# Splitting the tokens of a mixture of experts into two short-mantissa parts, and reordering the work inside an expert

## Chip, cores and metric

One core of a Trainium2 chip runs the whole program. The metric is the device time of one execution in microseconds (us). The kernel before takes 1766.9 us, the median of three runs (1766.51 to 1769.05 us).

## What is computed

The program is two transformer blocks on 256 tokens of 1024 numbers. The change lies in the mixture of experts (MoE) of the first block. Cut to what matters here, with `T` = 256, `D` = 1024, 32 experts and 4 of them for each token:

```
h      = rms_norm(x) * gain + shift
logits = h @ w_router + b_router
top 4 experts of each token, gates = softmax of their logits
for each expert e, on the tokens that chose it:
    u = h[those] @ w_mlp1[e] + b_mlp1[e]           # 1024 x 2048
    a = min(u[even], 7) * sigmoid(1.702 * ...) * (clip(u[odd]) + 1)
    y = a @ w_mlp2[e] + b_mlp2[e]                  # 1024 x 1024
    out[those] += gate * y
x = x + gt2 * rms_norm(out)
```

An expert's weights are 12 MB, so the MoE streams 384 MB from memory.

## The kernel before, in words

All of it is one function whose instructions run on each engine in the order in which the code issues them; semaphores alone tie the engines together. TensorE (PE) multiplies, VectorE (DVE) and ScalarE (ACT) evict and do elementwise work, GpSimd (POOL) does little, and SyncE (SP) issues the weight loads.

**Weights.** They come in chunks of 1 MB, twelve for an expert: `("m1", e, k)` for k = 0 to 7 and `("m2", e, q)` for q = 0 to 3. In the MoE a list of 18 buffers holds them (`NA` 4, `NE1` 2, `ND` 4, `NC` 3, `NF2` 4, and the buffer `xb` once the transposed tokens `x1` are read, L1332). `done(key)` (L121) hands a buffer back and issues the next load at once; SP waits there until the buffer's last reader is through.

**Routing (L1309 to L1385).** The tokens are turned, the router's logits and the top 4 are found, and `q1` says for each token and expert in which of 64 slots (`CAP`) of that expert the token sits. `select` (L1213) makes 0/1 matrices from it on DVE.

**Gather.** For a group of experts, `gather_rows` (L1227) multiplies the selection, already scaled by the tokens' norm `yt` (`factored`, L1220), by the tokens `x_tok` in float32: two PSUM banks of 512 columns. `gather_half` (L1239) copies a bank on ACT, turns it with four PE transposes, and evicts with gain and shift on ACT and DVE into `xg`, two pairs of evictions for each expert. The groups are expert 0 alone (by `gather_few`, L1261), then pairs 1 and 2, 3 and 4, and so on, and expert 31 alone (L1291). Expert e does the gather of the next group when it is the last of its own (`look`), so the experts with an even number do it.

**One expert (L1540 to L1654).** In the order of PE: the bias (`up_start`); products with chunks 0 to 2 of m1, both halves `u0` and `u1` of the result (`up(0, ..)`, `up(1, ..)`); `spread`, which adds the rows of the expert before to the output; chunk 3; with `look` the gather's products; chunk 4 of both halves; the first half of the turned gather; chunks 5 to 7 of `u0`; the second half of the gather; chunks 5 to 7 of `u1`. In float32 every product of the code is two instructions on PE, and the 64-column tiles run two at a time. Then `glu` (L1423) makes `a_sb` of `u0` on DVE and ACT, `slots_of` (L1404) finds which tokens the rows belong to, `turn` (L1436) transposes `a_sb` and ACT copies it to `aT`, `glu` does `u1`, and `down_q` (L1442) multiplies by the four chunks of m2.

**Experts with more than 64 tokens.** Three conditional blocks (`tc.If(more > 0)`, L1580, L1624, L1640) do the rest; here two experts, 3 and 17, take them. Where a block isn't taken, each engine still passes it in its order, and there sets the semaphores that the block's instructions would have set. The tile `vx` (L1579) of the first two blocks, read on DVE in the second, and the tile `aT` (L1627) share one buffer:

```
            vx = P.tile([128, 512], F32, name="vx", tag="aT", bufs=1)
            ...
            glu(us, a_sb)
            ax = P.tile([128, 1, 256], F32, name="ax", tag="sely", bufs=1)
            with tc.If(more > 0):
                nc.vector.tensor_tensor(vx, vx, up_more(range(4, KD)), op=OP.add)
                glu([vx], ax)
            aT = P.tile([128, 512], F32, name="aT", tag="aT", bufs=1)
```

Of the kernel before, what the change touches and what calls it, by code (L numbers as in the profile page):

```python
# [10 lines left out]
F32 = mybir.dt.float32  # L11
F32R = mybir.dt.float32r
# [3 lines left out]
AF = mybir.ActivationFunctionType  # L16
OP = mybir.AluOpType
# [4 lines left out]
D = 1024  # L22
KD = D // 128
NE = 32
CAP = 64
MORE = 32
# [4 lines left out]
GB = 2  # L31
# [5 lines left out]
ND = 4  # L37
NF2 = 4
IN2 = (8, 0, 9, 1, 6, 2, 7, 3, 4, 5)
# [7 lines left out]
def body(ctx: ExitStack, tc: tile.TileContext, I, out, dbg=None, n_experts=NE):  # L47
    nc = tc.nc
# [31 lines left out]
    def wps(name):  # L80
        if len(banks) == 1:
            return banks["w"].tile([128, 512], F32, name=name, tag="w")

        tags = banks["tags"]
        tags.append(tags.pop(0))
        return banks["w"].tile([128, 512], F32, name=name, tag=tags[-1], bufs=1)
# [1117 lines left out]
    with ExitStack() as ph:  # L1204
# [14 lines left out]

        def factored(sel, w):  # L1220

            ys = P.tile([128, 2, w], F32, name="sely", tag="selz" if w == MORE else "sely", bufs=1)
            for b in range(2):
                nc.vector.tensor_scalar(ys[:, b], sel[:, b].bitcast(F32), yt[:, b:b + 1], None, op0=OP.mult)
            return ys

        def gather_rows(sel, w):  # L1227

            ys = factored(sel, w)
            ps = []  # L1230
            for q in range(2):
                p = wps("xrp")
                for b in range(2):
                    nc.tensor.matmul(p[0:w, :], ys[:, b], x_tok[:, b, q * 512:(q + 1) * 512], start=(b == 0),  # L1234
                                     stop=(b == 1), skip_group_check=True)
                ps.append(p)
            return ps

        def gather_half(ps, q, w, xgs):  # L1239

            xr = P.tile([128, 512], F32, name="xr", tag="yh", bufs=1)
            nc.scalar.activation(xr[0:w, :], ps[q][0:w, :], AF.Copy)  # L1242
            p = ps[q]
            for c in range(4):
# [16 lines left out]
        def gather_few(sel, w, xg):  # L1261

            ys = factored(sel, w)
            n = 128 // w
            m = D // n
            p = wps("xrp")
            for b in range(2):
                for g in range(n):
                    nc.tensor.matmul(p[w * g:w * g + w, 0:m], ys[:, b], x_tok[:, b, g * m:(g + 1) * m],
                                     start=(b == 0), stop=(b == 1), skip_group_check=True, tile_position=(0, w * g))  # L1270
            xr = P.tile([128, 512], F32, name="xr", tag="yh", bufs=1)
# [18 lines left out]

        groups = [[0]] + [list(range(e, min(e + GB, n_experts))) for e in range(1, n_experts, GB)]  # L1291

        def group_size(gi):
            return len(groups[gi])
# [36 lines left out]
        dump("x1T", x1)  # L1331
        slots.append((xpool, "xb", state["moe_end"]))  # L1332
        rt = P.tile([128, 2, NE], F32, name="rt", tag="aT")
# [37 lines left out]
        xg0 = group_tile(0)  # L1371
        gather_few(sel0[:, :, 0], CAP, xg0[0])
        cur = sel0, xg0
# [29 lines left out]

        def slots_of(e, sel, w, tg, sg):  # L1404

            pm = wps("pm")
            for b in range(2):
                for c in range(128 // w):
                    nc.tensor.matmul(pm[w * c:w * c + w, 0:2], sel[:, b, :].bitcast(F32), gt2[:, b, e, :],
                                     start=(b == 0), stop=(b == 1), skip_group_check=True, tile_position=(0, w * c))  # L1410
            nc.vector.tensor_copy(tg, pm[:, 0:2])
            nc.vector.tensor_scalar(sg, iota_t, pm[:, 0:1], None, op0=OP.is_equal)
# [79 lines left out]
        def next_slots(e, q, done):  # L1492

            nc.vector.tensor_scalar(q[:, :, e:e + 1], q[:, :, e:e + 1], -float(done), None, op0=OP.add)
            sel = select(lambda b: q[:, b, e:e + 1][:, :, None], 1, MORE, "selx", 1)[:, :, 0]
            slots_of(e, sel, MORE, tgx, sgx)
            gather_few(sel, MORE, xgx)
# [42 lines left out]
        for e in range(n_experts):  # L1540
            gi, j = (e + GB - 1) // GB, (e + GB - 1) % GB if e else 0
            look = e == groups[gi][-1] and gi + 1 < ng
# [47 lines left out]

            kb = KD - 1 if e == n_experts - 1 else 5
            for k in range(4, kb):
                up(0, (k,))
                up(1, (k,))
            if look:
                gather_half(xrs, 0, w, nxg)
            up(0, range(kb, KD))
            if look:
                gather_half(xrs, 1, w, nxg)
            up(1, range(kb, KD))  # L1600
            if e == min(BIAS_AT, n_experts - 1):
# [19 lines left out]
            sg = P.tile([128, T], F32R, name="sg", tag="sg", bufs=1)  # L1621
            glu(us, a_sb)
            ax = P.tile([128, 1, 256], F32, name="ax", tag="sely", bufs=1)
# [4 lines left out]
            for k in range(4, KD):  # L1628
                done(("m1", e, k))
            slots_of(e, sel[:, :, j], CAP, tg, sg)  # L1630
            pt = wps("apt")
            turn(a_sb, (0,), aT, pt)
            glu(us, a_sb, (1,))
            yp = wps("yp")
# [396 lines left out]
```

## Time and profile before

| | us |
|---|---|
| median of three runs | 1766.9 |
| the profiled execution | 1763.47 |
| its span, first to last instruction | 1761.7 |
| MoE, first product with w_mlp1 to last product with w_mlp2 | 193.0 to 1175.2 |
| PE busy in the span | 1641.9 (93%) |
| DVE, ACT, POOL busy | 682.7, 516.2, 17.3 |

Engine times are from one profiled execution, counted from its first instruction. PE's busy time is the time in which at least one matmul runs; matmuls overlap, so a busy PE can still have room. "Granted clock" (PEclk) is the share of full TensorE clock: 1.00 is 2.4 GHz, 0.50 is 1.2 GHz.

### The profile page before, as it was taken

The page shows a single profiled execution, that of the slowest core. Times are in us where ns is not written, and L with a number is a line of the kernel's source. Part 1 is how long each engine was busy: PE and PEld are TensorE (multiplying, and loading weights), DVE is VectorE, ACT ScalarE, POOL GpSimd, SP SyncE. Part 2 cuts the span into 40 slices and gives each one's busy share as a digit, 9 for nine tenths or more (in the row PEclk, how much of TensorE's full clock was granted, in tenths as well). Part 3 has the DMA queues.
Part 4 walks back from the last instruction along what each step waited for, and adds up shares of the span by engine and source line. Part 5 has one row for each costly group of instructions (what it writes and reads, how often), then busy time and mean ns, then how long its engine had stood idle before and what let it go on. Part 6 is the DMA issues. An engine that isn't in the chain of part 4 may idle for free. (4 is left out here: it accounts for less than half of the span.)

```text
span 1761.7 us, 25407 instructions
## 1 busy us (share of the span) xinstructions
PE 1641.9 (93%) x9983; PEld 975.6 (55%) x9983; DVE 682.7 (39%) x1444; ACT 516.2 (29%) x980; POOL 17.3 (1%) x37
## 2 busy tenths in 40 slices
PE   6998899899999799989999999979999999999997
PEld 3776332333333233233333333339999998999997
DVE  4656312212221121221212121237666765666666
ACT  2544201101110111110111011135444546554443
POOL 1000000000000000000000000000000000000000
PEclk8999899999999899999999999989999999999999
DMA  9987899799999999979999999955565653445552
GB/s 324 371 262 291 347 412 402 289 411 413 416 413 415 406 415 415 409 308 412 413 416 413 416 414 415 416 192 168 168 201 166 205 182 121 144 154 193 188 171 96
DMA packets 169750, 545.61 MB, mean 310 GB/s; under 512 B 11280, under 2 KB 90720, under 8 KB 133728
## 3 DMA queue, kind: packets, MB, share of 16 engines
q1 hardware_dynamic: 168304, 540.60, 79.9%
q8 instruction: 125, 2.05, 0.5%
q0 software_dynamic: 480, 1.58, 0.3%
q10 hardware_dynamic: 784, 0.92, 0.2%
q14 instruction: 57, 0.47, 0.1%
HBM read 542.01 MB, written 1.05 MB: 308 GB/s over the span
## 5 line engine op out<-in xcount | busy, mean ns | idle before, releaser
L1551 PE MATMUL u<-chunk,xg 128*64 128x512 f32 x2048 | 471.6, 602 | 2.2 <-PEq L1580 1.9
L1551 PEld LDWEIGHTS u<-chunk,xg 128*64 128x64 f32 x2048 | 145.7, 138 | 267.9 <-issue 253.9
L1455 PE MATMUL yp<-chunk,aT 128*64 128x512 f32 x1024 | 250.2, 633 | 18.2 <-ACT aT L1440 14.9
L448 DVE TENSOR_TENSOR ul<-chunk,uh 128x1024 fp32r<-128x1024 f32 x202 | 239.1, 1220 | 36.1 <-ACT uh L434 35.7
L434 ACT ACTIVATE uh<-chunk 128x1024 fp32r<-128x1024 f32 x202 | 205.0, 1049 | 58.7 <-DMA chunk<-in_ffn_w_up_dram 31.0
L310 PE MATMUL gu<-nhi,uh 128*128 128x256 f32 x704 | 200.1, 284 | 0.0
L310 PE MATMUL gu<-nhi,ul 128*128 128x256 f32 x704 | 199.5, 283 | 0.0
L310 PE MATMUL gu<-nlo,uh 128*128 128x256 f32 x704 | 199.5, 283 | 0.0
L1455 PEld LDWEIGHTS yp<-chunk,aT 128*64 128x64 f32 x1024 | 70.7, 142 | 147.2 <-issue 123.4
L310 PEld LDWEIGHTS gu<-nhi,uh 128*128 128x128 f32 x704 | 135.5, 192 | 1.2 <-issue 0.4
L310 PEld LDWEIGHTS gu<-nlo,uh 128*128 128x128 f32 x704 | 135.4, 192 | 0.9
L310 PEld LDWEIGHTS gu<-nhi,ul 128*128 128x128 f32 x704 | 135.4, 192 | 0.0
L1465 DVE SCALAR_TENSOR_TENSOR yl<-yp,tg,yh 128x512 fp32r<-128x512 f32 x32 | 24.0, 751 | 243.4 <-ACTq L1580 185.2
L1256 DVE TENSOR_TENSOR xg<-xrp,gs 128x128 f32<-128x128 f32 x62 | 18.1, 292 | 254.9 <-ACT xg L1251 254.9
L1430 DVE TENSOR_SCALAR g<-u 128x256 f32<-128x256 f32 x64 | 26.9, 420 | 190.1 <-PE u L1551 190.1
L1431 ACT ACTIVATE s<-g 128x256 f32<-128x256 f32 x66 | 27.5, 417 | 222.5 <-DVE g L1430 219.2
L1464 ACT ACTIVATE yh<-yp,tg 128x512 fp32r<-128x512 f32 x32 | 22.0, 687 | 164.1 <-PEq L1640 147.4
L1242 ACT ACTIVATE xr<-xrp 128x512 f32<-128x512 f32 (+1 forms) x32 | 19.0, 594 | 168.2 <-PE xrp L1234 168.2
L1251 ACT ACTIVATE xg<-xrp,modT,gs 128x64 f32<-128x64 f32 x124 | 43.3, 399 | 84.7 <-PE xrp L1245 73.9
L1440 ACT ACTIVATE aT<-apt 128x256 f32<-128x256 f32 x64 | 24.5, 383 | 143.2 <-PE apt L297 106.1
L1234 PE MATMUL xrp<-x_tok,sely 128*128 128x512 f32 (+1 forms) x128 | 58.7, 601 | 5.0 <-PEq L1580 5.0
L1142 DVE TENSOR_TENSOR gu<-gu,rs 128x512 f32<-128x512 f32 (+1 forms) x46 | 30.7, 668 | 82.7 <-PE gu L310 82.4
(465 smaller groups left out, 2331.0 us busy)
## 6 DMA issues: line engine op xcount, KB each, us to landing
chunk<-in_w_mlp_dram SPq DMA_DIRECT2D x384, 1024.0 KB, 18.9
chunk<-in_w_ada_dram SPq DMA_DIRECT2D x24, 1024.0 KB, 6.8
chunk<-in_ffn_w_gate_dram SPq DMA_DIRECT2D x22, 1024.0 KB, 5.4
chunk<-in_ffn_w_up_dram SPq DMA_DIRECT2D x22, 1024.0 KB, 7.9
chunk<-in_ffn_w_down_dram SPq DMA_DIRECT2D x22, 1024.0 KB, 6.2
chunk<-in_w_in_dram SPq DMA_DIRECT2D x17, 1024.0 KB, 5.0
chunk<-in_w_gate_dram SPq DMA_DIRECT2D x8, 1024.0 KB, 6.7
chunk<-in_w_out_dram SPq DMA_DIRECT2D x6, 1024.0 KB, 8.4
```

Of the source, the lines that this page charges most:

```text
L310: nc.tensor.matmul(ps, a, b, start=first, stop=False, skip_group_check=True)
L434: nc.scalar.activation(hi if spec is None else spec(hi), view(raw(key)), AF.Copy)
L448: nc.vector.tensor_tensor(vl, view(raw(key)), vh.bitcast(F32), op=OP.subtract)
L1142: nc.vector.tensor_tensor(gu[:, a0:a1, :], p, rs[:, None, :].to_broadcast([128, a1 - a0, T]), op=OP.mult)
L1234: nc.tensor.matmul(p[0:w, :], ys[:, b], x_tok[:, b, q * 512:(q + 1) * 512], start=(b == 0), stop=(b == 1), skip_group_check=True)
L1251: nc.scalar.activation(xg[:, k, :], at, AF.Identity, scale=gs[:, 2, k:k + 1], bias=modT[:, 24 + k:25 + k])
L1430: nc.vector.tensor_scalar(g, uv[:, :, 0], 7.0, None, op0=OP.min)
L1431: nc.scalar.activation(s, g, AF.Sigmoid, scale=1.702)
L1440: nc.scalar.activation(aT[:, r * 256:(r + 1) * 256], pt[:, r * 256:(r + 1) * 256], AF.Copy)
L1455: nc.tensor.matmul(yp[w * d:w * d + w, 0:m], a, wt[:, o:o + m], start=(q + h == 0), stop=(q + h == 4), skip_group_check=True, tile_positio ...
L1465: nc.vector.scalar_tensor_tensor(yl, yp[:, 0:m], tg[:, 1:2], yh.bitcast(F32), op0=OP.mult, op1=OP.subtract)
L1551: nc.tensor.matmul(u, xg[j][:, k, :], raw(("m1", e, k))[:, n * 512:(n + 1) * 512], start=False, stop=(k == KD - 1), skip_group_check=True, ...
```

## The change

Once the router has read them, the tokens are split: `x_hi` is a copy rounded to the short mantissa (F32R) made on ACT, and `x_lo` is the rest, subtracted on POOL. `gather_rows` takes the plain 0/1 selection times both parts, one instruction for each product, and fetches the norm `yt` of each row with tiny products; ACT multiplies by it in its copy. `gather_few` takes both parts as float32. The groups become pairs from expert 0 on, so that the first pair is gathered before the loop, and experts 1, 3, ... 29 do the others; nobody gathers in expert 30. `x_tok` gives its buffer `xa` to the weight chunks (but for the last 14), `x_hi` lies in `xb`, `NF2` falls to 3, and in the last expert POOL adds the parts to `x_tok` again. Inside an expert chunks 4 and 5 of `u0` go before the first half of the gather, chunks 6 and 7 before the second, and chunks 4 to 7 of `u1` behind it; both halves of `glu` stand before the second conditional block; and `slots_of` stands behind `turn`, in a bank of its own.

```diff
-NF2 = 4
+NF2 = 3
...
         def gather_rows(sel, w):
-            ys = factored(sel, w)
             ps = []
             for q in range(2):
                 p = wps("xrp")
-                for b in range(2):
-                    nc.tensor.matmul(p[0:w, :], ys[:, b], x_tok[:, b, q * 512:(q + 1) * 512], start=(b == 0),
-                                     stop=(b == 1), skip_group_check=True)
-                ps.append(p)
+                if q == 0:
+                    for b in range(2):
+                        nc.tensor.matmul(p[0:w, 0:1], sel[:, b].bitcast(F32), yt[:, b:b + 1], start=(b == 0),
+                                         stop=(b == 1), skip_group_check=True)
+                    yg = P.tile([128, 1], F32, name="yg", tag="yg", bufs=2)
+                    nc.vector.tensor_copy(yg[0:w, :], p[0:w, 0:1])
+                    ps.append(yg)
+                    first = p
+                else:
+                    for n, pn in ((1, p), (0, first)):
+                        for b in range(2):
+                            for x in (x_hi, x_lo):
+                                nc.tensor.matmul(pn[0:w, :], sel[:, b], x[:, b, n * 512:(n + 1) * 512],
+                                                 start=(b == 0 and x is x_hi), stop=(b == 1 and x is x_lo),
+                                                 skip_group_check=True)
+                    ps += [p, first]
             return ps
...
-            nc.scalar.activation(xr[0:w, :], ps[q][0:w, :], AF.Copy)
-            p = ps[q]
+            nc.scalar.activation(xr[0:w, :], p[0:w, :], AF.Copy, scale=yg[0:w, :])
...
-        groups = [[0]] + [list(range(e, min(e + GB, n_experts))) for e in range(1, n_experts, GB)]
+        groups = [list(range(e, min(e + GB, n_experts))) for e in range(0, n_experts, GB)]
...
-        slots.append((xpool, "xb", state["moe_end"]))
+        x_hi = xpool.tile([128, 2, D], F32R, name="x_hi", tag="xb")
+        x_lo = P.tile([128, 2, D], F32R, name="x_lo")
+        for h in (1, 0):
+            for b in range(2):
+                cs = slice(h * 512, (h + 1) * 512)
+                nc.scalar.activation(x_hi[:, b, cs], x_tok[:, b, cs], AF.Copy)
+                nc.gpsimd.tensor_tensor(x_lo[:, b, cs], x_tok[:, b, cs], x_hi[:, b, cs].bitcast(F32), op=OP.subtract)
+        slots.append((xpool, "xa", state["moe_end"] - 14))
...
-        gather_few(sel0[:, :, 0], CAP, xg0[0])
+        w = group_size(0) * CAP
+        xrs = gather_rows(sel0, w)
+        for h in range(2):
+            gather_half(xrs, h, w, xg0)
...
-            kb = KD - 1 if e == n_experts - 1 else 5
-            for k in range(4, kb):
-                up(0, (k,))
-                up(1, (k,))
-            if look:
-                gather_half(xrs, 0, w, nxg)
-            up(0, range(kb, KD))
-            if look:
-                gather_half(xrs, 1, w, nxg)
-            up(1, range(kb, KD))
+            if e == n_experts - 1:
+                for k in range(4, KD):
+                    up(0, (k,))
+                    up(1, (k,))
+                x_tok = xpool.tile([128, 2, D], F32, name="x_tok", tag="xa")
+                for b in range(2):
+                    nc.gpsimd.tensor_tensor(x_tok[:, b, :], x_hi[:, b, :].bitcast(F32), x_lo[:, b, :].bitcast(F32),
+                                            op=OP.add)
+            else:
+                up(0, (4, 5))
+                if look:
+                    gather_half(xrs, 0, w, nxg)
+                up(0, (6, 7))
+                if look:
+                    gather_half(xrs, 1, w, nxg)
+                up(1, range(4, KD))
...
-            glu(us, a_sb)
+            glu(us, a_sb, (0, 1))
             ax = P.tile([128, 1, 256], F32, name="ax", tag="sely", bufs=1)
             with tc.If(more > 0):
...
-            slots_of(e, sel[:, :, j], CAP, tg, sg)
             pt = wps("apt")
             turn(a_sb, (0,), aT, pt)
-            glu(us, a_sb, (1,))
+            pm = banks["w"].tile([128, 512], F32, name="pm", tag="u0")
+            slots_of(e, sel[:, :, j], CAP, pm)
+            slot_rows(pm, tg, sg)
             yp = wps("yp")
             down_q(yp, CAP, raw(("m2", e, 0)), 0, aT)
             turn(a_sb, (1,), aT, pt)
```

## Rows read from the trace of the kernel before

**Rows 1.** The profile page, part 1: busy us, share of the span, instructions.

```profile
PE 1641.9 (93%) x9983; PEld 975.6 (55%) x9983; DVE 682.7 (39%) x1444; ACT 516.2 (29%) x980; POOL 17.3 (1%) x37
```

**Rows 2.** Windows: us, busy (instructions) by engine, PEclk, DMA share, GB/s; experts 5, 6, 30.

```profile
359.50:384.90 25.40, 24.23 (x120) 8.49 (x120) 4.30 (x11) 2.29 (x5) 0.00 (x0) 1.00 1.01 405
384.90:418.00 33.10, 30.96 (x136) 10.44 (x136) 7.42 (x23) 6.13 (x15) 0.00 (x0) 0.95 1.01 415
...
1115.90:1145.70 29.80, 28.73 (x136) 9.70 (x136) 6.06 (x19) 4.75 (x11) 0.00 (x0) 1.00 1.02 416
```

**Rows 3.** Lines 112 (1078 to 1079 us) and 1551 (1115 to 1117 us): durations, starts.

```profile
L112 SPq DMA_DIRECT2D chunk<-in_w_mlp_dram x1: 3879/3879/3879, 1078.4 to 1078.4; - x1
...
DMA to landing us min/median/max: 21.3/21.3/21.3
...
L1551 PE MATMUL u<-chunk,xg x4: 592/592/592, 1116.3 to 1116.8; 128*64 128x512 f32 x4
```

**Rows 4.** Timeline of PE, expert 6, which gathers: start us, us, what.

```profile
393.99 3.67 PE L1234 MATMUL xrp<-x_tok,sely 128*128 128x512 f32 x8 [0.31 <-PEq L1580]
...
399.46 0.66 PE L1245 MATMUL xrp<-ident,xr 128*128 128x128 f32 x4
...
402.77 0.66 PE L1245 MATMUL xrp<-ident,xr 128*128 128x128 f32 x4
403.36 2.80 PE L1551 MATMUL u<-chunk,xg 128*64 128x512 f32 x12
...
408.66 3.56 PE L1455 MATMUL yp<-chunk,aT 128*64 128x512 f32 x8 [0.47 <-ACT aT L1440]
```

**Rows 5.** Timelines of ACT and DVE, the same expert.

```profile
401.81 0.59 ACT L1242 ACTIVATE xr<-xrp 128x512 f32<-128x512 f32 x1
...
405.79 0.42 DVE L1430 TENSOR_SCALAR g<-u 128x256 f32<-128x256 f32 x1
...
408.22 0.38 ACT L1440 ACTIVATE aT<-apt 128x256 f32<-128x256 f32 x1 [1.56 <-PE apt L297]
```

**Rows 6.** Lines 1624 and 1440, 400 to 410 us: waits of the queues (q).

```profile
L1624 DVEq EVENT_SEMAPHORE  x1: 21/21/21, 407.6 to 407.6; - x1
...
L1440 ACTq EVENT_SEMAPHORE  x1: 17/17/17, 407.7 to 407.7; - x1
```

**Rows 7.** Timeline of PE, expert 7, which does not gather.

```profile
426.98 7.09 PE L1551 MATMUL u<-chunk,xg 128*64 128x512 f32 x32 [0.16 <-PEq L1580]
...
435.75 1.94 PE L1455 MATMUL yp<-chunk,aT 128*64 128x512 f32 x8 [0.53 <-ACT aT L1440]
```

**Rows 8.** Timeline of PE and line 1036: short-mantissa products and their weight loads.

```profile
168.31 0.39 PE L1036 MATMUL y<-u,mixl 128*128 128x512 f32 x1
...
168.99 0.39 PE L1036 MATMUL y<-u,mixl 128*128 128x512 f32 x1
...
L1036 PEld LDWEIGHTS y<-u,mixl x32: 187/188/192, 146.8 to 170.8; 128*128 128x128 f32 x32
```

**Rows 9.** Windows over the second products of experts 2 and 4.

```profile
272.23:281.40 9.17, 9.17 (x34) 2.60 (x34) 0.99 (x3) 0.71 (x2) 0.00 (x0) 0.83 1.02 421
...
351.78:359.40 7.62, 7.61 (x34) 2.33 (x34) 1.00 (x3) 0.71 (x2) 0.00 (x0) 1.00 1.02 426
```

**Rows 10.** The start of the MoE (window, timeline), and POOL beside DVE at the end.

```profile
183.30:190.10 6.80, 4.14 (x13) 1.03 (x12) 2.52 (x14) 0.18 (x1) 0.00 (x0) 0.50 1.02 423
...
186.19 3.68 PE L1269 MATMUL xrp<-x_tok,sely 128*64 128x512 f32 x8 [1.73 <-DVE sely L1224]
...
193.03 1.48 PE L1551 MATMUL u<-chunk,xg 128*64 128x512 f32 x6
...
1754.35 1.44 POOL L1975 TENSOR_TENSOR o_tok<-x,fgain 128x512 f32<-128x512 f32 x1 [2.40 <-DVE x L1969]
...
1754.57 1.76 DVE L1975 TENSOR_TENSOR o_tok<-x,fgain 128x512 f32<-128x512 f32 x1
```

**Rows 11.** Groups by line and form: the gather for the experts with more tokens.

```profile
L1269 PE MATMUL xrp<-x_tok,sely 128*32 128x256 f32 x32 | 2.1, 385 | 1.4 <-DVE sely L1224 1.4
```

More of the change, by code (lines that the diff above doesn't have):

```diff
@@ L1218, in select @@
             return sel
-        def factored(sel, w):
-            ys = P.tile([128, 2, w], F32, name="sely", tag="selz" if w == MORE else "sely", bufs=1)
-            for b in range(2):
-                nc.vector.tensor_scalar(ys[:, b], sel[:, b].bitcast(F32), yt[:, b:b + 1], None, op0=OP.mult)
-            return ys
         def gather_rows(sel, w):
-            ys = factored(sel, w)
             ps = []
@@ L1232, in gather_rows @@
                 p = wps("xrp")
-                for b in range(2):
-                    nc.tensor.matmul(p[0:w, :], ys[:, b], x_tok[:, b, q * 512:(q + 1) * 512], start=(b == 0),
-                                     stop=(b == 1), skip_group_check=True)
-                ps.append(p)
+                if q == 0:
[14 more added lines that the diff above has]
+                    ps += [p, first]
             return ps
         def gather_half(ps, q, w, xgs):
+            yg, p = ps[0], ps[1 + q]
+            q = 1 - q
             xr = P.tile([128, 512], F32, name="xr", tag="yh", bufs=1)
-            nc.scalar.activation(xr[0:w, :], ps[q][0:w, :], AF.Copy)
-            p = ps[q]
+            nc.scalar.activation(xr[0:w, :], p[0:w, :], AF.Copy, scale=yg[0:w, :])
             for c in range(4):
@@ L1261, in gather_few @@
         def gather_few(sel, w, xg):
-            ys = factored(sel, w)
+            ys = P.tile([128, 2, w], F32, name="sely", tag="selz", bufs=1)
+            for b in range(2):
+                nc.vector.tensor_scalar(ys[:, b], sel[:, b].bitcast(F32), yt[:, b:b + 1], None, op0=OP.mult)
             n = 128 // w
@@ L1267, in gather_few @@
             for b in range(2):
-                for g in range(n):
-                    nc.tensor.matmul(p[w * g:w * g + w, 0:m], ys[:, b], x_tok[:, b, g * m:(g + 1) * m],
-                                     start=(b == 0), stop=(b == 1), skip_group_check=True, tile_position=(0, w * g))
+                for x in (x_hi, x_lo):
+                    for g in range(n):
+                        nc.tensor.matmul(p[w * g:w * g + w, 0:m], ys[:, b], x[:, b, g * m:(g + 1) * m].bitcast(F32),
+                                         start=(b == 0 and x is x_hi), stop=(b == 1 and x is x_lo),
+                                         skip_group_check=True, tile_position=(0, w * g))
             xr = P.tile([128, 512], F32, name="xr", tag="yh", bufs=1)
@@ L1401, in o_part, with slots_of @@
             return o_ps[2 * b + h][:, c:c + m]
-        def slots_of(e, sel, w, tg, sg):
-            pm = wps("pm")
+        def slots_of(e, sel, w, pm):
             for b in range(2):
@@ L1410, in slots_of, with slot_rows @@
                                      start=(b == 0), stop=(b == 1), skip_group_check=True, tile_position=(0, w * c))
+        def slot_rows(pm, tg, sg):
             nc.vector.tensor_copy(tg, pm[:, 0:2])
@@ L1495, in next_slots @@
             sel = select(lambda b: q[:, b, e:e + 1][:, :, None], 1, MORE, "selx", 1)[:, :, 0]
-            slots_of(e, sel, MORE, tgx, sgx)
+            pm = wps("pm")
+            slots_of(e, sel, MORE, pm)
+            slot_rows(pm, tgx, sgx)
             gather_few(sel, MORE, xgx)
@@ L1540, in body @@
         for e in range(n_experts):
-            gi, j = (e + GB - 1) // GB, (e + GB - 1) % GB if e else 0
+            gi, j = divmod(e, GB)
             look = e == groups[gi][-1] and gi + 1 < ng
@@ L1589, in body @@
                 ahead = nsel, nxg
-            kb = KD - 1 if e == n_experts - 1 else 5
-            for k in range(4, kb):
-                up(0, (k,))
-                up(1, (k,))
-            if look:
-                gather_half(xrs, 0, w, nxg)
-            up(0, range(kb, KD))
-            if look:
-                gather_half(xrs, 1, w, nxg)
-            up(1, range(kb, KD))
+            if e == n_experts - 1:
[3 more added lines that the diff above has]
+                x_tok = xpool.tile([128, 2, D], F32, name="x_tok", tag="xa")
+                for b in range(2):
+                    nc.gpsimd.tensor_tensor(x_tok[:, b, :], x_hi[:, b, :].bitcast(F32), x_lo[:, b, :].bitcast(F32),
[8 more added lines that the diff above has]
+                up(1, range(4, KD))
             if e == min(BIAS_AT, n_experts - 1):
```

## The prediction, made before the change was run

> **What bounds the kernel now.** The page first: PE is busy 93% of the span [rows 1], but matmuls overlap, so that alone decides nothing. The windows of single experts do [rows 2]. An expert that doesn't gather takes 25.4 us and one that gathers for two takes 33.1 us, so a pair takes 58.5 us, 29.25 us an expert. Its weights, twelve chunks of 1.049 MB, take 30.3 us at 415 GB/s, with the DMA engines full [rows 2]. So the DMA is the slower of the two, and PE still doesn't wait for it, because it lives off a store of chunks loaded ahead: the first chunk of expert 30 (the 361st of 384 issues) was issued at 1078.4, landed 21.3 us later, and was first used at 1116.3 [rows 3], 16.6 us after it had landed. Hence two rules for this change: each microsecond that PE's order loses in an expert is lost, and of what it gains only some 16 us can be kept before the DMA holds PE.
>
> Then the timeline of a gathering expert [rows 4, 5]. The gather's products start at 393.99; the second products (`down_q`) start at 408.66, 14.67 us later. The first products end at 406.16, so PE has 2.5 us there with some 0.8 us of small work. What ends it is a chain: the last evictions of the gather keep DVE, only behind them `glu` starts (405.79), the conditional block is passed on DVE at 407.6, ACT's wait ahead of `aT` ends at 407.7 [rows 6], the copy takes 0.38 us. That wait of ACT is for DVE to be through the block, since `aT` lies in the buffer of `vx`, which the block reads on DVE. In an expert that doesn't gather, the first products end at 434.07 and the second start at 435.75 [rows 7], 1.69 us (1.6 in most).
>
> **The change, part by part.**
>
> *Both halves of `glu` ahead of the block.* DVE passes the block only when it has done the second half, and that waits for the last product of `u1`. A `glu` takes from 405.79 to 407.6 [rows 5, 6], 1.85 us with the pass. Without a gather: last product, 1.85, then 0.05 until ACT goes, 0.38 for the copy [rows 5], some 0.1 of semaphores: 2.4 us instead of 1.62, so +0.78 in each of 17 experts (the even ones and 31): **+13.3**. `slots_of`, moved behind `turn`, fills this gap and costs nothing; the rows that it finds on DVE are needed only in the next expert. `turn` of the second half and the second chunk's products stand behind the first `down_q`, 1.9 us of PE work, which hides them.
>
> *Gathering experts.* The gather's products: today 8 instructions of 0.427, 3.41 us. Afterwards 8 of a short mantissa; three of those follow each other in 0.68 us [rows 8], so 1.8 us, and 0.35 for the norms' four tiny products: 2.2. Then, from the gather's start: chunks 4 and 5 of `u0` (1.75) bring the first transposes to 3.95. From first transposes to the second copy's end took 399.46 to 402.40 [rows 4, 5], 2.95 us, so the second transposes come at 6.95, after 0.65 us in which PE has nothing, since only 1.75 us of products stand between now. From there to the first `glu` 3.0 (402.77 to 405.79): 10.0. Two `glu` of 1.85, copy and semaphores 0.5: `down_q` at 14.2 instead of 14.67. PE's saving of 1.2 us is eaten by the second `glu`. Fifteen such experts, -0.47 each: **-7.0**. PE then idles from 11.0 to 14.2.
>
> The price of the short-mantissa products hangs on their weight loads being hidden: a load of 128 columns takes 0.19 us [rows 8], and yet the products start every 0.227 us. The Trainium skill (TensorE: Matmul & The Clock Gate, "Part 3: Packing small matmuls") says that a weight load overlaps with matmuls in flight only where the row group differs; here all eight use all rows, and by that each pair would take some 0.4 us, 1.5 us more for a gather, and the sum would be 22 us higher. The row has full-height products too, so I take the row.
>
> *Expert 30 gathers no more:* 29.8 to 25.4 [rows 2], **-4.4**.
>
> *Start.* The first pair's gather stands before the loop, behind the split. Today the gather for expert 0 starts at 186.19, after 1.73 us of waiting for the scaled selection [rows 10]; unscaled, it can start about 1 us earlier, an estimate. At half clock (0.50 there [rows 10]) norms and products take 3.9 us, to 189.1; 2.95 to the second transposes and some 2.3 to the first expert's last eviction give first products at 194.4 against 193.03 [rows 10]: +1.4 (with full clock about -0.2). The copies of `x_hi` go beside the router on ACT, which waits for PE then: nothing; uncovered they'd be 4 times 0.59, by the copy of [rows 5]. The four subtractions of `x_lo` on POOL, up to 1.44 us each [rows 10], lie beside the route's chain and end before the last products need them. But POOL can hold DVE: at the kernel's end a DVE operation with two inputs took 1.76 us beside a POOL one that ended at 1755.79 [rows 10], so it was through 0.54 us after POOL let go. The route's chain on DVE runs just then, so this costs between 0 and 5.8; I take 2.1, for not all of its operations have two inputs. Start: **+3.5**, from -0.2 to 7.2.
>
> The Trainium skill (SBUF — State Buffer, "SBUF: two separate sides") has the shared ports locked for a whole instruction, and only against DVE operations with two SBUF inputs or in a two-port mode. By that the four with two inputs (both `oh`, both `sel`) would wait for one POOL operation each at most, and in the mean for half of it, 2.9 us by an estimate from the row, which leaves the sum about where it is.
>
> *`gather_few` with two parts* doubles 2.1 us [rows 11]: **+2.1**.
>
> *Buffers.* 17 instead of 18 (16 for the last 14 chunks) take one or two chunks of 2.5 us from the store of 16.6; what is left covers it: 0. SP waits for `xa` until POOL has subtracted, with loads queued behind it, but the store is full then. POOL's sums for `x_tok` in the last expert have its idle engine: 0; uncovered they'd cost 4 times 1.44.
>
> These make +7.5.
>
> *Clock.* In 10 of the 15 experts that gather for a pair, the second products start at 1.2 GHz: expert 2 took 9.17 us for them with a granted clock of 0.83 in the mean, expert 4 took 7.62 at 1.00 [rows 9], so 1.6 us each. Thirteen of the 15 have the same gap of 2.5 us with 0.8 us of work; experts with 1.6 to 1.7 us are never caught. The change gives the others a gap of 2.4 us with the same work. No row shows that order, so 0 to 16 of 16 can be caught (0 to 26 us); by the nearest rows, the gathers', I take half: **+12.8**. The gathering ones get 3.2 us; the five that escaped may be caught (0 to 8), **+2**, since part of the slow stretch then falls into idle time.
>
> Sum: +22. The profiled execution had 1763.5, 3.4 us under the median; the runs' median stands for the next measurement, so 1766.9 + 22 = **1789 us**.
>
> **The rivals.**
>
> *Down to 1745: the second `glu` does not hold the copy.* If ACT's wait were already met by the first half, `down_q` would come 2.87 us after the last eviction (405.79 to 408.66 [rows 4, 5]), at 12.9 instead of 14.67: 15 times -1.75, -4.4 and +5.6 make -25, and the shorter gaps would lose the 10 slow stretches, another -16. Of these 41 the DMA leaves what its store and fewer full buffers give, about 22. For it: the first `turn` needs the first half alone. Against: ACT's wait ended 0.1 us after DVE was through the block [rows 6].
>
> *1775: as forecast, but the clock keeps up,* because the small work now lies together at the gap's beginning: +8.
>
> *1808: the clock falls in nearly every expert:* 7.5 + 26 + 8.
>
> *1767: the parts cancel.* If DVE gets through the evictions earlier than today, the whole 1.24 us of a gather come through (-18.6 instead of -7.0), and a few slow stretches give it back.
>
> **How the numbers follow.** A measurement can tell about 0.2% (3.5 us) from no change. Forecast, with some stretches slow: 0.50. Clock keeps up: 0.13. Falls everywhere: 0.12. Second `glu` doesn't hold: 0.15. Cancelling: 0.10, over both sides of the line. So faster 0.16, same 0.11, slower 0.73. The range leaves out the 1745 case and the ends of the others: 1764 to 1811; it takes in most of the start's bounds and nearly all of the clock's.
>
> **What would show it.** Right: ACT's wait ahead of the first `aT` ends with DVE's second `glu`; 2.4 us from first to second products without a gather, some 3.2 with one; gather products of 2.2 us; even experts at 26 to 28 us; more windows of second products at 0.82; first products near 196; no wait of PE for chunks. Wrong: the first copy to `aT` starting before the second `glu` ends; PE waiting for chunks late in the MoE; gaps below 1.7 us.

## The result, and the profile after

The changed kernel takes 1791.6 us (median of 4 runs, 1790.4 to 1797.2); the kernel before, run between them, 1766.7. The ratio is 1.0147, with an interval of 1.0122 to 1.0173: 25 us slower, with 1789 forecast and 1764 to 1811 as the range. The profiled execution took 1790.4, its span is 1788.7 against 1761.7 before, so 27.0 us are to be found.

The page has PE busy for less time than before [rows 1], in a longer span: the time went into idle PE, not into work.

```profile
PE 1631.0 (91%) x10067; PEld 996.7 (56%) x10067; DVE 682.5 (38%) x1424; ACT 521.6 (29%) x983; POOL 27.1 (2%) x43
```

The groups of instructions by line say what PE idles for (busy us, mean ns | idle just before, its releasers). `u` are the first products and their weight loads, `yp` the second ones:

```profile
L1477 PE MATMUL yp<-chunk,aT 128*64 128x512 f32 x1024 | 252.0, 636 | 48.4 <-ACT aT L1462 48.4
...
L1575 PEld LDWEIGHTS u<-chunk,xg 128*64 128x64 f32 x2048 | 156.2, 138 | 256.4 <-issue 247.0 <-DMA chunk<-in_w_mlp_dram 5.6 <-DMA chunk<-in_ffn_w_gate_dram 0.3
```

and the second products before:

```profile
L1455 PE MATMUL yp<-chunk,aT 128*64 128x512 f32 x1024 | 250.2, 633 | 18.2 <-ACT aT L1440 14.9 <-issue 3.3
```

The second products wait 48.4 us for ACT's copy to `aT`, where they waited 14.9 us for it before. For chunks the weight loads of the first products wait 5.6 us only (7.9 before): the smaller store of chunks cost nothing.

Windows by expert, as in [rows 2]: expert 9, which gathers, expert 10, which doesn't, and expert 30 (us, busy by engine, PEclk, DMA share, GB/s).

```profile
494.90:526.60 31.70, 28.15 (x142) 10.87 (x143) 7.20 (x22) 6.33 (x16) 0.00 (x0) 1.00 0.97 389
526.60:553.00 26.40, 24.22 (x122) 8.80 (x123) 4.39 (x11) 2.29 (x6) 0.00 (x0) 1.00 1.00 403
...
1144.90:1171.30 26.40, 24.19 (x122) 8.81 (x123) 4.39 (x11) 2.29 (x6) 4.58 (x2) 1.00 1.02 416
```

An expert without a gather takes 1.0 us more than before, and expert 30, which gathers no more, 3.4 us less. A gathering expert at full clock takes 31.7.

**The gap.** The timeline of expert 26 between its first and second products (start us, us, what, idle before and its releaser):

```profile
1044.67 0.42 DVE L1452 TENSOR_SCALAR g<-u 128x256 f32<-128x256 f32 x1 [1.64 <-PE u L1575]
...
1044.93 0.41 PE L297 MATMUL apt<-ident,a_sb 128*128 128x128 f32 x2 [0.30 <-PEq L1655]
...
1045.27 0.40 PE L1428 MATMUL pm<-gt,sel 128*64 128x2 f32 x8
...
1046.10 0.43 DVE L1456 SCALAR_TENSOR_TENSOR a_sb<-a_sb,g 128x256 f32<-128x256 f32 x1
...
1046.68 0.38 ACT L1462 ACTIVATE aT<-apt 128x256 f32<-128x256 f32 x1 [1.07 <-DVEq L1655]
...
1047.11 1.94 PE L1477 MATMUL yp<-chunk,aT 128*64 128x512 f32 x8 [1.44 <-ACT aT L1462]
```

Read from the bottom: the second products wait for the copy, and the copy for DVE's queue at line 1655, the conditional block. The transposes that the copy reads were through at 1045.34. DVE reaches the block only at 1046.53, when it has done the second half of `glu`. From the last first product to the first second one it is 2.48 us, against 1.59 to 1.70 before [rows 7].

In expert 27, which gathers, PE's timeline has the same chain behind a shorter gather:

```profile
1064.10 0.58 PE L1227 MATMUL xrp<-rqy,sel 128*128 128x1 f32 x4 [0.31 <-PEq L1604]
...
1065.09 0.39 PE L1237 MATMUL xrp<-x_hi,sel 128*128 128x512 f32 x1
1065.32 0.39 PE L1237 MATMUL xrp<-x_lo,sel 128*128 128x512 f32 x1
...
1068.41 0.66 PE L1250 MATMUL xrp<-ident,xr 128*128 128x128 f32 x4
...
1071.49 0.66 PE L1250 MATMUL xrp<-ident,xr 128*128 128x128 f32 x4 [0.56 <-ACT xr L1248]
...
1078.84 1.51 PE L1477 MATMUL yp<-chunk,aT 128*64 128x512 f32 x6 [1.66 <-ACT aT L1462]
```

The gather takes 2.44 us of PE (1064.10 to 1066.54, where `u` goes on) in place of 3.61 (393.99 to 397.60, where it went on before), but 0.56 us is lost at the second transposes and 0.61 in the gap (3.11 for 2.50), and the second products start 14.74 us after the gather's start. Before it was 14.67 [rows 4].

**The start.** The timeline of the route, after:

```profile
182.34 5.15 POOL L1348 TENSOR_TENSOR x_lo<-x_tok,x_hi 128x512 fp32r<-128x512 f32 x4 [2.96 <-ACT x_hi L1347]
...
183.70 2.64 DVE L1365 TENSOR_TENSOR oh<-iota_e,if 128x128 f32<-128x128 f32 x2
...
187.49 0.49 DVE L1216 TENSOR_TENSOR sel<-slot,q 128x128 fp32r<-128x128 f32 x2
...
199.30 1.07 PE L1575 MATMUL u<-chunk,xg 128*64 128x512 f32 x2
```

and the same operations before:

```profile
183.12 0.49 DVE L1348 TENSOR_TENSOR oh<-iota_e,if 128x128 f32<-128x128 f32 x2
...
184.75 0.36 DVE L1216 TENSOR_TENSOR sel<-slot,q 128x64 fp32r<-128x64 f32 x2
```

The first product comes at 199.30 against 193.03 [rows 10]. Of these 6.3 us, 0.6 were lost ahead of the split (`oh` starts that much later), 2.15 while DVE's two `oh` stood beside POOL's subtractions, and 3.5 between `sel` and the first product (8.3 before, 11.8 after): the gather for a pair, with its products at 1.2 GHz (a granted clock of 0.50 from 187.5 to 192.3), and the first expert's bias products, which run at 1.2 GHz too (0.50 from 196.3 to 203.0).

**The clock.** Windows over the second products of experts 1, 2, 24 and 25:

```profile
249.70:258.90 9.20, 9.18 (x34) 2.57 (x34) 0.00 (x0) 0.38 (x1) 0.00 (x0) 0.81 1.03 423
277.70:286.90 9.20, 9.19 (x34) 2.59 (x34) 0.00 (x0) 0.38 (x1) 0.00 (x0) 0.81 1.03 420
...
988.90:996.50 7.60, 7.52 (x34) 2.33 (x34) 0.06 (x1) 0.41 (x2) 0.00 (x0) 1.00 1.02 405
1020.80:1028.40 7.60, 7.51 (x34) 2.22 (x34) 0.00 (x0) 0.38 (x1) 0.00 (x0) 1.00 1.03 412
```

Early in the MoE the second products run partly at 1.2 GHz (9.2 us, as in [rows 9]), later they don't: ten experts are caught (1, 2, 4 to 8, 13, 14, 19), none from 20 to 30, though their gaps are the same. Before it was ten too (2, 6, 8, 12, 14, 16, 20, 22, 26, 28). Expert 31, the last, is caught in both and is not counted.

### The profile page after: what moved, and what is told of

The parts are those of the page before. It is cut to its first block, busy times and chain, and to the rows that moved or that the text cites. A ratio compares the mean times of both kernels' runs of the same rounds, so it can differ in the third digit from the quotient of the medians.

```text
span 1788.7 us, 25600 instructions
## 1 busy us (share of the span) xinstructions
PE 1631.0 (91%) x10067; PEld 996.7 (56%) x10067; DVE 682.5 (38%) x1424; ACT 521.6 (29%) x983; POOL 27.1 (2%) x43
## 5 line engine op out<-in xcount | busy, mean ns | idle before, releaser
L1575 PE MATMUL u<-chunk,xg 128*64 128x512 f32 x2048 | 473.4, 604 | 2.7 <-PEq L1604 2.4
L1575 PEld LDWEIGHTS u<-chunk,xg 128*64 128x64 f32 x2048 | 156.2, 138 | 256.4 <-issue 247.0
L1477 PE MATMUL yp<-chunk,aT 128*64 128x512 f32 x1024 | 252.0, 636 | 48.4 <-ACT aT L1462 48.4
L434 ACT ACTIVATE uh<-chunk 128x1024 fp32r<-128x1024 f32 x202 | 205.2, 1049 | 59.5 <-DMA chunk<-in_ffn_w_up_dram 26.4
L1248 ACT ACTIVATE xr<-xrp,yg 128x512 f32<-128x512 f32 x32 | 22.0, 686 | 145.1 <-PE xrp L1237 145.1
L297 PEld LDWEIGHTS apt<-ident,a_sb 128*128 128x128 f32 x128 | 13.8, 149 | 77.9 <-issue 55.8
```

The source lines that it names most:

```text
L434: nc.scalar.activation(hi if spec is None else spec(hi), view(raw(key)), AF.Copy)
L1477: nc.tensor.matmul(yp[w * d:w * d + w, 0:m], a, wt[:, o:o + m], start=(q + h == 0), stop=(q + h == 4), skip_group_check=True, tile_positio ...
L1575: nc.tensor.matmul(u, xg[j][:, k, :], raw(("m1", e, k))[:, n * 512:(n + 1) * 512], start=False, stop=(k == KD - 1), skip_group_check=True, ...
```

## The experiments

Theory H was the prediction's: the copy to `aT` waits until DVE is through the conditional block, and so for every `glu` that stands ahead of the block. Rivals were the order of gather and half-products (O), ACT's own order (A), the start, and the clock. The runs of the kernel before beside the first four had a median of 1766.8, beside the next three 1764.7, beside the last two 1768.0.

**1. The second half of `glu` taken from ahead of the block to behind the turn of the first half.**

```diff
-            glu(us, a_sb, (0, 1))
+            glu(us, a_sb)
...
             turn(a_sb, (0,), aT, pt)
+            glu(us, a_sb, (1,))
             pm = banks["w"].tile([128, 512], F32, name="pm", tag="u0")
```

> The second half of glu goes back behind the conditional block and the first turn; all else stays as changed. Theory H (the second half, ahead of the block, holds ACT's copy to aT): the time from the last first product to the first second product falls from 2.48 us to some 1.4 us without a gather and from 3.11 us to some 1.9 us with one, 17 x 1.05 + 15 x 1.2 = 36 us less, and the slow stretches at 1.2 GHz get rarer; the DMA gives back a part, since only some 18 us of chunks are in store: 1745 to 1765 us. Rival O (the order of gather and half-products costs the time): within 5 us of the changed kernel, 1786 to 1797 us.

Measured: 1743.9 us, ratio to before 0.987 (0.984 to 0.990). One line's place turns 25 us slower into 23 us faster. The timeline of expert 26:

```profile
996.11 0.41 PE L297 MATMUL apt<-ident,a_sb 128*128 128x128 f32 x2 [0.30 <-PEq L1655]
...
996.61 0.38 ACT L1462 ACTIVATE aT<-apt 128x256 f32<-128x256 f32 x1 [3.32 <-DVE a_sb L1454]
...
997.05 1.51 PE L1477 MATMUL yp<-chunk,aT 128*64 128x512 f32 x6 [0.20 <-ACT aT L1462]
```

The copy goes 0.09 us after the transposes are through (996.52), and `glu`'s second half runs beside the second products. (The row names a DVE operation that ended just then, at 996.60; in expert 27 it names the transposes.) The gap is 1.24 us without a gather and 1.60 with one, and experts take 25.2 and 30.2 us. Only expert 8 has second products at 1.2 GHz; in its gap lie the products that add the bias `b_mlp2`, and it is 6.0 us long. H holds, O falls, and the time lies 1 us below the range that H gave. One thing is new: first products wait for the DMA.

```profile
L1575 PEld LDWEIGHTS u<-chunk,xg 128*64 128x64 f32 x2048 | 153.6, 138 | 265.7 <-issue 235.5 <-DMA chunk<-in_w_mlp_dram 26.3
```

**2. The kernel before with both halves ahead of the block, and nothing else.**

```diff
-            glu(us, a_sb)
+            glu(us, a_sb, (0, 1))
...
-            glu(us, a_sb, (1,))
```

> The kernel before with one part of the change alone: both halves of glu ahead of the block. Theory H: 2.4 us instead of 1.6 us between first and second products without a gather (16 x 0.8 = 13 us), some 4.3 us instead of 2.5 us with one (16 x 1.85 = 30 us): 1805 to 1822 us, more than the whole change cost. Rival O: 1764 to 1772 us, as before.

Measured: 1842.0 us, ratio 1.043 (1.041 to 1.046). The direction is H's, the size some 20 us more than expected. The gaps are 2.97 us without a gather (2.4 expected) and 4.46 to 4.72 with one. The timeline of expert 19 shows what the expectation left out:

```profile
864.10 0.42 DVE L1434 SCALAR_TENSOR_TENSOR a_sb<-a_sb,g 128x256 f32<-128x256 f32 x1
...
864.73 0.41 PE L297 MATMUL apt<-ident,a_sb 128*128 128x128 f32 x2 [1.39 <-DVEq L1624]
...
865.18 0.38 ACT L1440 ACTIVATE aT<-apt 128x256 f32<-128x256 f32 x1 [1.56 <-DVEq L1639]
...
865.61 1.94 PE L1455 MATMUL yp<-chunk,aT 128*64 128x512 f32 x8 [0.47 <-ACT aT L1440]
```

In the old order the transposes too are released by DVE's pass of the block, so turn and copy stand one behind the other after it. In the changed kernel the turn is ahead of the slot products and is through by then. So the other place of the slot products, behind the turn and in a bank of their own, seems a gain of its own, of 0.5 us here (6 tests it). Most of the rest is clock: with gaps this long the second products of every expert that gathers for others are slow, 8.8 to 10.3 us, and all second products together are busy for 271.0 us in place of 250.2.

**3. The second half right behind the block, ahead of the turn.**

```diff
-            glu(us, a_sb, (0, 1))
+            glu(us, a_sb)
...
                 glu([vx], ax)
             aT = P.tile([128, 512], F32, name="aT", tag="aT", bufs=1)
             for k in range(4, KD):
                 done(("m1", e, k))
+            glu(us, a_sb, (1,))
             pt = wps("apt")
             turn(a_sb, (0,), aT, pt)
```

> As changed, but the second half of glu stands right behind the conditional block, still ahead of the first turn. It tells what holds ACT's copy. Theory H (the pass of the block on DVE): the copy needs only ACT's own sigmoid of the second half before it, so some 1.5 us without a gather and 2.2 us with one, and 1748 to 1768 us. Rival A (ACT's order: the copy stands behind the second sigmoid and needs all of the second half): 2.3 us or more without a gather, 1780 to 1795 us.

Measured: 1748.1 us, ratio 0.990 (0.988 to 0.992). Here ACT has the sigmoid of the second half ahead of the copy, as rival A wanted it, and DVE has nothing of it ahead of the block. The timeline of expert 26:

```profile
1007.22 0.42 ACT L1453 ACTIVATE s<-g 128x256 f32<-128x256 f32 x1 [3.08 <-DVE g L1452]
...
1007.54 0.36 ACT L1462 ACTIVATE aT<-apt 128x256 f32<-128x256 f32 x1
...
1007.96 1.51 PE L1477 MATMUL yp<-chunk,aT 128*64 128x512 f32 x6 [0.27 <-ACT aT L1462]
```

The gap is 1.30 us, and 2.05 with a gather. The price of ACT's order is 0.06 and 0.45 us; A falls.

**4. The split without its low part:** `x_lo` is set to zero once, ahead of the route, and POOL subtracts nothing. The low part of the gathered tokens is left out.

```diff
+        x_lo = P.tile([128, 2, D], F32R, name="x_lo")
+        nc.gpsimd.memset(x_lo.bitcast(F32), 0.0)
...
-                nc.gpsimd.tensor_tensor(x_lo[:, b, cs], x_tok[:, b, cs], x_hi[:, b, cs].bitcast(F32), op=OP.subtract)
```

> As changed, but the low parts x_lo are set to zero ahead of the router instead of being subtracted on POOL, so the gathered tokens and the residual are those of the high part alone. Theory L (POOL's subtractions hold DVE's operations with two inputs): the two operations that make oh take 0.5 us instead of 2.64 us, the first product of the MoE starts 2.1 us earlier or more, the time falls by 2 to 4 us. Rival (the later start is the pair's gather alone): oh and the time stay.

Measured: 1799.4 us, ratio 1.017 (1.014 to 1.021): 8 us slower than the changed kernel, with less work. What it was made for it shows, in the timeline of DVE:

```profile
184.53 0.49 DVE L1365 TENSOR_TENSOR oh<-iota_e,if 128x128 f32<-128x128 f32 x2
```

`oh` is back to 0.49 us, so POOL's subtractions were what held it. Theory L's 2 to 4 us did not come, and the run can't tell the price of the start, for two reasons. The router already ran at half clock in it (granted 0.50 from 176.5 to 183.5, 0.80 in the changed kernel), and the first product came only 0.7 us earlier. And the second products of 19 experts are slow instead of ten (without expert 8, 18 instead of nine); windows of experts 24 and 25, which weren't caught in the changed kernel:

```profile
991.70:1000.90 9.20, 9.17 (x34) 2.57 (x34) 0.00 (x0) 0.38 (x1) 0.00 (x0) 0.81 1.03 416
1025.10:1034.30 9.20, 9.13 (x34) 2.50 (x34) 0.00 (x0) 0.39 (x1) 0.00 (x0) 0.81 1.02 421
```

The gaps are 2.48 and 3.11 us as there. So whether a gap of that length is caught is decided by something else than its length. The MoE of this run differs in a start 0.7 us earlier and in low parts that are zero; no run parts the two.

**5. The gap filled:** the changed kernel with four products that change no value, ahead of the slot products of every expert.

```diff
             pm = banks["w"].tile([128, 512], F32, name="pm", tag="u0")
+            for _ in range(4):
+                nc.tensor.matmul(pm, oh3[:, 0:1].to_broadcast([128, 128]), b13[:, 0:512], start=True, stop=True,
+                                 skip_group_check=True)
             slots_of(e, sel[:, :, j], CAP, pm)
```

> The kernel after, with four products of 128x512 into the idle bank of pm ahead of the slot products of every expert; they change no value and fill 0.9 us of the gap of 2.48 or 3.11 us between the first and the second products. Theory C (the slow stretches at the head of the second products are set off by PE's idle time in the gap): the 9 us slow second products of experts 1, 2, 4, 5, 6, 7, 14 and 19 go to 7.6, the gaps stay at 2.48 and 3.11, and the time falls by 8 x 1.6 = 13 us or somewhat more to 1772-1782. Rival R (the stretches come and go with a rhythm that has nothing to do with the gap): as many slow second products as before, and 1787-1795. Rival Q (the filler itself holds up the second products): gaps above 3 us and over 1800.

Measured: 1772.5 us, ratio 1.0036 (1.0023 to 1.0049), 19 us under the changed kernel, for more work. The timeline of expert 27, and windows over the second products of experts 1 and 2:

```profile
1060.21 1.03 PE L1665 MATMUL pm<-b,oh 128*128 128x512 bf16 x4
...
1062.37 1.08 PE L1477 MATMUL yp<-chunk,aT 128*64 128x512 f32 x4 [0.80 <-ACT aT L1462]
```

```profile
251.50:259.10 7.60, 7.50 (x34) 2.21 (x34) 0.00 (x0) 0.38 (x1) 0.00 (x0) 1.00 1.03 422
277.90:285.50 7.60, 7.51 (x34) 2.21 (x34) 0.00 (x0) 0.39 (x1) 0.00 (x0) 1.00 1.04 417
```

The gaps are still 2.48 and 3.12 us, and of the experts with no further tokens one (5) has slow second products. Gaps of the same length with 0.9 us less of idle PE in them go from 9 slow experts of 28 to one, which is what theory C said; rivals R and Q had other times. A lucky shift is not quite excluded: the first product comes 1.8 us later here, and experiment 4 shows that the count can change with the gaps as they are. But the ten executions all lie between 1769.7 and 1774.4 us, clear of the eight of the two unfilled kernels (1790.4 to 1801.5). The price of the falls in the changed kernel was at least 18 us (spans 1788.7 and 1770.7). Seven experts at 1.6 us or more are 12 to 13 of it (expert 5 stayed slow); the rest lies in experts 3, 8, 13, 17, 18 and 31, less the 1.8 us of the later start.

**6. The kernel before with the slot products alone moved behind the turn and the second `glu`;** gathers and tokens as before.

```diff
...
-            slots_of(e, sel[:, :, j], CAP, tg, sg)
             pt = wps("apt")
             turn(a_sb, (0,), aT, pt)
             glu(us, a_sb, (1,))
+            pm = banks["w"].tile([128, 512], F32, name="pm", tag="u0")
+            slots_of(e, sel[:, :, j], CAP, pm)
+            slot_rows(pm, tg, sg)
```

> The kernel before (f32 gathers, no short-mantissa parts), with the slot products and their rows alone moved behind the turn of the first half and the second glu. Theory G (the new place of the slot products helps only where ACT's wait is not the last to end, so the rest of the gain of the kernel with the glu behind the turn comes from the gather): gaps of 1.25 us in place of 1.62 in the experts that don't gather, 2.2-2.5 in those that do, 16 x 0.37 = 6 us, and 0 to 16 us more if slow second products vanish: 1743-1761, likeliest 1757. Rival S (the order of the slot products is the whole gain): gaps of 1.25 and 1.6, no slow second products, and 1744 or less, since the start stays as early as before.

Measured: 1759.5 us, ratio 0.996 (0.994 to 0.998). Theory G holds, which had 1757 as likeliest; S falls. Without a gather the gap is 1.23 us, with one 2.46, where the timeline of expert 26 shows why the new place helps nothing there:

```profile
1022.21 0.42 DVE L1436 SCALAR_TENSOR_TENSOR a_sb<-a_sb,g 128x256 f32<-128x256 f32 x1
...
1022.78 0.41 PE L297 MATMUL apt<-ident,a_sb 128*128 128x128 f32 x2 [1.58 <-DVEq L1628]
```

The transposes go when DVE has done the evictions of the gather, `glu`, and the block. So of the 23 us of experiment 1 the place of the slot products gives some 5. The rest, by difference (no run has the new gather alone), comes with the other parts, the gather above all: with it the first `glu` starts 1.2 us ahead of the end of the first products (experiment 1, expert 27) instead of 0.4 [rows 4, 5], which shortens the gap, and with the short gaps the slow second products are gone too.

**7. The kernel of experiment 1 with the 15 gathers inside the loop left out;** every expert multiplies the tokens gathered for the first pair, so the output is another.

```diff
-                xrs = gather_rows(nsel, w)
-                nxg = group_tile(gi + 1)
+                nxg = xg
...
-                if look:
-                    gather_half(xrs, 0, w, nxg)
...
```

> The kernel with the first glu alone ahead of the block and the second behind the turn (1743.9 us), with the 15 gathers inside the loop left out: every expert multiplies the tokens gathered for the first pair. That takes about 5 us of PE work out of each of 15 experts, 75 us. Theory D (that kernel has come down to the DMA: 384 chunks at about 415 GB/s less the store): the time falls by no more than 15 us, to 1730-1744, and PE's waits for chunks grow from some 33 us to 90 or more. Rival P (PE still sets the end): 1670-1690, waits little changed.

Measured: 1735.6 us, ratio 0.982 (0.980 to 0.984): 15 experts less 5.0 us each (30.2 and 25.2 in experiment 1), 75 us of PE's time, give 8 us. The row of the first products' weight loads (26.3 us for chunks in experiment 1), and a window late in the MoE:

```profile
L1575 PEld LDWEIGHTS u<-chunk,xg 128*64 128x64 f32 x2048 | 157.1, 141 | 354.9 <-issue 232.8 <-DMA chunk<-in_w_mlp_dram 115.9
```

```profile
950.00:1100.00 150.00, 128.19 (x600) 40.83 (x596) 22.31 (x59) 10.87 (x25) 4.67 (x2) 0.97 1.01 413
```

The DMA engines are full and PE waits, as theory D said. The kernel of experiment 1 has come within 8 us of what the DMA allows with this start.

**8. The kernel of experiment 1 with the start of before:** expert 0 alone is gathered from the unsplit tokens, the split follows, and the pairs are (1, 2), (3, 4) and so on.

```diff
-        groups = [list(range(e, min(e + GB, n_experts))) for e in range(0, n_experts, GB)]
+        groups = [[0]] + [list(range(e, min(e + GB, n_experts))) for e in range(1, n_experts, GB)]
...
-        w = group_size(0) * CAP
-        xrs = gather_rows(sel0, w)
-        for h in range(2):
-            gather_half(xrs, h, w, xg0)
+        gather_few(sel0[:, :, 0], CAP, xg0[0], (x_tok,))
+        x_hi = xpool.tile([128, 2, D], F32R, name="x_hi", tag="xb")
...
```

> The kernel with the second glu behind the turn (1743.9 us), with the start of the kernel before: expert 0 alone is gathered from the unsplit tokens ahead of the loop, the split into two parts comes behind that, and the pairs are (1, 2), (3, 4) and so on again, so that expert 30 gathers for 31 once more. Theory T (the late first product costs its whole length, since the DMA stands still with a full store from about 194 to 211 us, and the later wait for chunks comes from that): first u product near 194-195 us in place of 200.9, the DMA idle only some 10 us there, the waits of PE for chunks no more than 33 us, and 1736-1740, 4 to 7 us under the other. Rival U (PE bound; the gather added in expert 30 costs 5 us and eats it): 1742-1746. Rival V (the split beside the first expert holds up DVE's evictions for it): first product later than 197.

Run beside it, experiment 1 once more:

> The kernel with the second glu behind the turn once more, beside the one with the early start on the same chip: 1740-1747, first u product near 200.9.

Measured: 1740.0 us, ratio 0.985 (0.983 to 0.987), and 1744.6 for the other. It is the fastest that computes all. Windows from 195 to 210 us say where the 4.5 us come from (DMA share and GB/s stand last); first the kernel of experiment 1, then this one:

```profile
195.00:210.00 15.00, 12.52 (x46) 4.07 (x48) 4.14 (x16) 5.72 (x11) 0.00 (x0) 0.77 0.06 22
```

```profile
195.00:210.00 15.00, 14.58 (x64) 5.52 (x62) 3.83 (x12) 3.55 (x8) 4.12 (x4) 0.90 0.55 203
```

With its store full the DMA stands still until first products free a chunk. The first product comes at 194.8 here, at 200.9 there. What a late start costs is DMA time, and in a MoE that the DMA ends, it is lost. Not all of the 6 us came through: PE waits 35.1 us for chunks in this run, a little over the 33 that theory T allowed.

## Why the prediction was right

The sum was +22, the runs' medians differ by 24.9, the profiled spans by 27.0. Its main step held: the second half of `glu`, ahead of the block, holds the copy. That the sum came so near is in good part luck, since the terms were off in both directions. Against the spans:

| term | forecast | measured | from |
|---|---|---|---|
| both halves of `glu` ahead of the block, 17 experts | +13.3 | about +15 | gap 2.48 less 1.6 |
| 15 gathering experts | -7.0 | about +3 | 31.7 at full clock; 31.5 for expert 10 before |
| expert 30 without a gather | -4.4 | -4.3 | 26.4 for 29.8, with 0.9 of `glu` counted above |
| start | +3.5 | +5.7 | 6.3 less the 0.6 that was late before the split |
| `gather_few` with two parts | +2.1 | about +3 | 5.0 us busy for 2.1 |
| clock | +14.8 | about +2 | second products busy 252.0 for 250.2; ten slow experts before and after, two of them slow for longer |

The measured terms make about +24.4. With the 0.6 that was late before the split, and first products that are busy 1.8 us longer (473.4 for 471.6), which no term had, it is 26.8 of the 27.0.

- **`glu` ahead of the block** is shown by both directions: taken away (1, 3) the gap falls to 1.24 and 1.30, put into the kernel before alone (2) it rises from 1.6 to 2.97. The prediction's reason, that `aT` lies in the buffer of `vx`, is argued from the code: no run gave `vx` a buffer of its own. The rival of 1745, that the second half doesn't hold the copy, had the right time for a kernel that takes that half away, and is wrong for this one.
- **The gathering experts** were mis-sized, by 0.6 us each. The step said that PE's saving of 1.2 us is eaten by the second `glu` down to 0.47. The order was right; the sizes were not: products and norms took 2.44 for 2.2, the first transposes came at 4.31 us for 3.95, the second ones at 7.39 for 6.95, and what had been lost by then was still lost at the second products (14.74 for 14.2). PE's wait at the second transposes was 0.56 for 0.65.
- **The weight loads** are hidden, as the trace said: the two products of the gather shown above start 0.23 us apart, and each has a load of 0.20 us:

```profile
L1237 PEld LDWEIGHTS xrp<-x_lo,sel 128*128 128x128 f32 x64 | 12.7, 198 | 2.1
L1237 PEld LDWEIGHTS xrp<-x_hi,sel 128*128 128x128 f32 x64 | 12.6, 197 | 2.7 <-ACT vx L1606 0.5
```

By the rule of the Trainium skill (TensorE: Matmul & The Clock Gate, "Part 3: Packing small matmuls"), as the prediction used it, a load and its product would have taken some 0.4 us together, an estimate; the measurement decides against it for these full-height products.

- **The start** was mis-sized. POOL's hold on DVE was 2.15 us for 2.1, both in `oh`; the `sel` came just as POOL ended (182.34 + 5.15 = 187.49) and lost nothing. The Trainium skill (SBUF — State Buffer, "SBUF: two separate sides") has such operations of DVE wait for a whole POOL instruction; the trace agrees (two `oh` take 2.64 us beside subtractions of 1.3 us each), and without the subtractions (4) they take 0.49. What was too small was the pair's gather: +1.4 forecast, +3.5 measured: products and norms took 4.4 for 3.9, the way to the second transposes 3.35 for 2.95, from there to the last eviction 2.8 for 2.3, and the first expert's bias products, at 1.2 GHz now, 0.85 for 0.43.
- **The clock** was mis-sized most, and terms elsewhere that had been put too low made up for it; that is the luck. The forecast let half of the experts that newly have a gap of 2.4 be caught, and more of the gathering ones than before. Of the first it was 4 of 15 with a gap of 2.48 (2, 4, 6, 14). And of the 13 gathering ones with no further tokens, five were caught, where nine had been before, although their gap had grown. The step took each expert for itself; the runs show that the falls come and go by stretches of experts, and that with the same gaps it was 18 of these 28 in experiment 4 and nine here.
- **Buffers at 0** was right: no waits for chunks worth naming. It stays right only while PE is slower than the DMA, as experiment 1 shows.

The slow second products by length of gap (without experts 3 and 17, which have further tokens, without 8, whose gap holds the bias, without 31, and in the kernel before, 2 and 6 without 0 and 30; of the kernel before and 6 only those that gather):

| gap, us | kernel | slow |
|---|---|---|
| 1.23 to 2.35 | 1 and 3 | none |
| 2.46 to 2.51 | before; 6 | 9 of 13; 6 of 13 |
| 2.47 to 2.53 | after; 4 | 4 of 15; 10 of 15 |
| 2.97 to 3.06 | 2 | 5 of 13 |
| 3.10 to 3.12 | after; 4 | 5 of 13; 8 of 13 |
| 4.46 to 4.72 | 2 | 13 of 13 |
| 2.48 to 2.54 and 3.12, filled | 5 | 1 of 28 |

**What stays open** is which of the gaps between 2.5 and 3.1 us are caught. The pattern holds for many experts in a row, and differs between two kernels with the same gaps whose first products come 0.7 us apart. A rhythm between the experts and the clock's falls is one guess; no run varied the length of a pair of experts alone. Open too is whether the copy would still wait if `vx` and `aT` had buffers of their own.

## What to carry to other kernels

A conditional block on an engine is a place in that engine's queue: here ACT's copy, which waits for DVE's pass of the block, waited for all that stood ahead of the block on DVE, also in the 30 experts that don't take it. So count, for each operation that moves across it, who waits behind the block, and put only the operations ahead whose results are needed there. A gain on PE's side is worth its price only as far as the DMA's store reaches (in experiment 7, 75 us less of PE's work gave 8); look at the DMA's idle time at the start of a stage before you trust it at the end.

## What had not been expected

- The same kernel with less work took 8 us more (4), and with 128 more products 19 us less (5): with gaps of 2.5 to 3.1 us, PE's clock is worth nearly as much as the whole change, and it can go either way with the gaps left as they are.
- A good order was one line away. With the second half behind the turn the change is 23 us faster than before instead of 25 slower, and with the old start 28 us faster (1740.0 against 1768.0).
- DMA engines that are full through the rest of the MoE stand nearly still for 15 us at its start (22 GB/s in the kernel of experiment 1), and that is where the last microseconds lay.
